# A two-layer hybrid decoder on one core: modulation sums by products with ones, a latent projection by quarters, and rotary halves exchanged by ScalarE copies

## The chip, the cores and the metric

The kernel runs on one core of one Trainium2 chip. The metric is the device time of one execution in microseconds (us); lower is better. The engines have these names in the profile: PE is TensorE (PEld its weight loads), DVE is VectorE, ACT is ScalarE, POOL is GpSimd, SP is SyncE, which here issues the DMAs.

## The reference: what is computed

A sequence of 256 rows of width 1024 passes two layers. Each layer is a token mixer and a SwiGLU feed-forward, both between RMS norms and modulated by shift, scale and gate vectors that come from one conditioning vector `c`:

```
c_act = jax.nn.silu(c)
for l in range(DEPTH):
    mod = c_act @ w_mod[l] + b_mod[l]
    sh_m, sc_m, g_m, sh_f, sc_f, g_f = jnp.split(mod, 6, axis=-1)
    h = rms_norm(x, mix_norm_pre[l]) * (1.0 + sc_m) + sh_m
    x = x + g_m * rms_norm(hybrid_mixer(h, ...), mix_norm_post[l])
    h = rms_norm(x, ffn_norm_pre[l]) * (1.0 + sc_f) + sh_f
    x = x + g_f * rms_norm(swiglu(h, ...), ffn_norm_post[l])
```

In the mixer one projection `h @ w_in` gives a latent of 256 columns (`cq`), attention keys and values, one index key, index weights, and the mLSTM parts. The normed latent is projected up to 8 query heads and 8 index-query heads of 64. An indexer scores all keys for each query, `sum_h w * relu(q_idx . k_idx)`, and only the 64 best causal keys take part in the softmax attention. A second head group is an mLSTM. Queries, keys, index queries and the index key are rotated:

```
x1, x2 = jnp.split(x, 2, axis=-1)
rope = concatenate([x1 * cos - x2 * sin, x2 * cos + x1 * sin], axis=-1)
```

The head width is 64, so each half has 32 elements, and the rotation needs the two halves exchanged.

## The kernel before, in words

Activations are held transposed: features on the 128 partitions, the 256 rows of the sequence along the free axis. The normed and modulated input of layer 0 is `n0hf` (8 blocks of 128 features), in full f32; from layer 1 on operands are split into two `fp32r` halves (names that end in `h` and `l`), and a product takes three passes.

**The prelude of layer 0.** The modulation vectors are matrix-vector products with 1024 x 6144 weights per layer (`w_mod`, 25 MB per layer). They are formed on DVE: `macc`, 128 partitions by n columns, gathers `w * c` over the 8 blocks of input features, and the sum over the partitions is left for PE. For the first norm the kernel does this by quarters q = 0..3 (`mod_quarter`): 8 loads of 256 KB each (tiles `wq`), 8 DVE operations of 128x512 (lines 206 and 208), then 4 PE transposes into a PSUM bank `pm`, a DVE reduce over it (line 218), an add of the bias (219), the scale vector `A` (220), two scalings that write two blocks of `n0hf` (line 965), and then the products `pvm` and `pva` of these two blocks, 16 of 128x512. Inside a quarter these steps are a chain, and PE waits on it.

**Mixer 0 after the prelude.** PE forms `m0pki` (index key, index weights and gates), `m0pcq` (the latent, 16 products), `m0kir` (rotated index key, by two products with the constant `dup`), `m0pwif`, `m0pgt` (gates), `m0pka` (attention keys), `m0pqidx` and `m0pq` (index queries, queries), the index scores `m0pi`, the logits `m0pl`. DVE rotates, computes the gates and the stabiliser scan `m0M`, goes on with the sums `macc` for the next modulation vectors (1 MB tiles `wm`, two 128x1024 operations each), adds up the scores `m0sc` and finds the 64th largest by rounds of MAX8 and MATCH_REPLACE8. ACT copies from PSUM, applies the relus `m0rl` and the exponentials. The first transposes of the attention weights, `m0pT`, need the exponentials, and these need the row maximum `m0mx`.

**Rotary.** `rope(dst, src, nm)` is called 6 times in each layer (names `rqidx0`, `rqidx1`, `rq0`, `rq1`, `rka0`, `rka1`), on a PSUM tile of 128 partitions (two heads of 64) by 512 columns:

```
xs = t2k(nm + "x"); copy(nm + "x", xs, src)         # ACT, PSUM to SBUF
pr = bankA(nm + "p"); matmul(pr, perm, xs)          # PE, halves exchanged and signed
dst = xs * cos                                       # POOL, or DVE
b = pr * sin; dst = dst + b                          # DVE (the add on POOL in two cases)
```

**Layer 1** has the same steps with three-pass products, with the later feed-forward blocks of PE work close behind. `row14p` are transposes that turn a gate vector into rows and do not belong to the rotary part.

**What sets the order.** The tile framework orders the instructions of each engine ahead of the run, by its own estimate of when each is ready; `issue_after` pins an operation behind another one. On the chip each engine then works through its list in that order, and an instruction that waits holds all behind it. SP issues the loads in order; SBUF tiles come from pools, and a load into a reused buffer waits for its last reader. PSUM banks come from two pools, `bankA` and `bankB`.

Of the kernel before, what the change touches and what calls it, by code (L numbers as in the profile page):

```python
# [56 lines left out]
def tile_hybrid_decoder(ctx: ExitStack, tc: tile.TileContext, a, out):  # L57
# [1006 lines left out]
```

## Time and profile before

| what | value |
|---|---|
| three runs | 734.39, 735.91, 737.62 us; median 735.91 us |
| the profiled execution, its own time | 736.93 us |
| span of the profiled execution | 735.2 us |
| PE busy | 702.1 us of it (95%) |
| DVE busy | 550.9 us (75%) |
| ACT busy | 348.3 us (47%) |
| POOL busy | 106.3 us (14%) |
| prelude, to the end of the last `pva` | about 58 us |
| mixer 0, from there to the first `m0pT` | about 60 us |
| from there to the start of layer 1's rotary part | about 306 us |
| layer 1's rotary part, to its first logits | about 40 us |

The span is counted from the first to the last instruction of the trace; the profiled execution has 1.73 us around it. Busy shares are averages over the program; the chain that ended last runs 80% through PE.

### The profile page before, as it was taken

Reading aid. Unit: us, or ns where it says so; the run is one execution under the profiler, and the core shown is the slowest. Engines: PE = TensorE matmul, PEld = TensorE weight load, DVE = VectorE, ACT = ScalarE, POOL = GpSimd, SP = SyncE. Lnnn points to the kernel's source line nnn. Section 1 sums busy time; section 2 is a strip of 40 time slices with the busy share of each in tenths; the row PEclk is TensorE's granted clock in tenths of the full one; section 3 lists DMA queues with packets and bytes.
Section 4 is the critical chain, followed back from the end, with each engine's and each line's share of the span. In section 5 each row is a group of like instructions: output and inputs, shape, how many; then the busy total and the mean of one; then the engine's idle time right before and its main releaser. Section 6 shows DMA issues by size and latency. Waiting matters only on the chain.

```text
span 735.2 us, 11619 instructions
## 1 busy us (share of the span) xinstructions
PE 702.1 (95%) x4581; PEld 618.8 (84%) x4581; DVE 550.9 (75%) x860; ACT 348.3 (47%) x613; POOL 106.3 (14%) x93
## 2 busy tenths in 40 slices
PE   2889999999999999999999989999999999999996
PEld 2337777888799999999988877999889999999995
DVE  4666989985998647897978899987776675655553
ACT  5112234665664444444536534685774444444442
POOL 1000420101000022210011263632210000000010
PEclk9999999999999999999999999999999999999999
DMA  9999953494958966989792933344536487664001
GB/s 305 355 297 386 367 208 104 159 329 156 315 211 303 332 217 230 339 295 340 257 370 90 329 118 115 121 150 131 181 135 228 164 303 260 215 207 172 1 1 57
DMA packets 106154, 162.77 MB, mean 221 GB/s; under 512 B 7586, under 2 KB 83950, under 8 KB 106100
## 3 DMA queue, kind: packets, MB, share of 16 engines
q1 hardware_dynamic: 106100, 162.04, 64.7%
q8 instruction: 36, 0.59, 0.3%
q14 instruction: 18, 0.15, 0.1%
HBM read 160.98 MB, written 1.05 MB: 220 GB/s over the span
## 4 chain that ended last, share of the span: by engine, by line
PE 80%; DVE 11%; ACT 3%; issue 3%; POOL 1%; DMA 1%; SPq 0%; DVEq 0%; POOLq 0%; ACTq 0%
PE f1pu L111 8%; PE f0pu L111 8%; PE f0pg L111 8%; PE f1pg L111 8%; PE f1y L111 7%; PE f0y L111 7%; PE m1pqk L111 3%; PE m1y L111 3%; PE pvm L111 3%; PE m0y L111 2%; PE pva L111 2%; PE m0pka L111 2%; PE m1pva L111 2%; PE m1pom L111 1%; PE m1pka L111 1%
## 5 line engine op out<-in xcount | busy, mean ns | idle before, releaser
L191 DVE SCALAR_TENSOR_TENSOR macc<-wm,ccol,macc 128x1024 f32<-128x1024 f32 x70 | 96.1, 1373 | 9.5 <-DMA wm<-in_w_mod_dram 8.8
L258 POOL TENSOR_TENSOR macc<-macc,br 1x512 f32<-1x512 f32 x6 | 10.0, 1666 | 166.6 <-DMA br<-in_b_mod_dram 166.6
L111 PE MATMUL m0pqk<-n0hf,m0wqk 128*128 128x256 f32 x128 | 29.6, 382 | 0.0
L111 PEld LDWEIGHTS m0pqk<-n0hf,m0wqk 128*128 128x128 f32 x128 | 23.8, 190 | 3.6 <-issue 0.5
L111 PE MATMUL pvm<-m0wvm,n0hf 128*128 128x512 f32 x32 | 18.5, 732 | 7.3 <-ACT n0hf L965 5.6
L208 DVE SCALAR_TENSOR_TENSOR macc<-wq,ccol,macc 128x512 f32<-128x512 f32 x28 | 21.0, 752 | 1.1
L111 PEld LDWEIGHTS pvm<-m0wvm,n0hf 128*128 128x128 f32 x32 | 7.1, 234 | 16.4 <-ACT n0hf L965 7.7
L965 ACT ACTIVATE n0hf<-n0xT,mod,A 128x256 f32<-128x256 f32 x7 | 3.9, 594 | 30.5 <-DVE A L220 30.5
L111 PE MATMUL m0pka<-n0hf,m0wka 128*128 128x256 f32 x64 | 16.0, 389 | 0.0
L111 PE MATMUL m0pom<-m0wom,n0hf 128*128 128x256 f32 x64 | 14.5, 379 | 0.0
L111 PE MATMUL pva<-m0wva,n0hf 128*128 128x512 f32 x32 | 14.4, 592 | 0.0
L111 PEld LDWEIGHTS m0pka<-n0hf,m0wka 128*128 128x128 f32 x64 | 11.5, 190 | 3.3 <-issue 1.6
L872 DVE TENSOR_TENSOR f1t<-f1pu,f1s 128x512 f32<-128x512 f32 x11 | 7.6, 692 | 7.5 <-PE f1pu L111 6.0
L111 PEld LDWEIGHTS m0pom<-m0wom,n0hf 128*128 128x128 f32 x64 | 11.9, 190 | 1.4
L262 POOL TENSOR_TENSOR ml<-macc,mh 128x512 fp32r<-128x512 f32 x6 | 9.5, 1586 | 24.0 <-ACT mh L260 24.0
L711 ACT ACTIVATE m0lm<-m0lm,m0mx 128x128 f32<-128x128 f32 (+1 forms) x16 | 7.1, 445 | 12.2 <-DVE m0mx L708 12.2
L111 PEld LDWEIGHTS pva<-m0wva,n0hf 128*128 128x128 f32 x32 | 6.1, 190 | 7.7 <-issue 7.7
L189 DVE TENSOR_SCALAR macc<-wm,ccol 128x1024 f32<-128x1024 f32 x10 | 8.8, 884 | 4.7 <-DMA wm<-in_w_mod_dram 3.5
L882 ACT CAST f0th<-f0t 128x512 fp32r<-128x512 f32 x10 | 6.2, 620 | 11.9 <-DVE f0t L872 11.9
L770 DVE SCALAR_TENSOR_TENSOR m1cv<-m1pqk,vc,m1cv 128x255 f32<-128x255 f32 (+2 forms) x24 | 11.1, 476 | 0.7 <-ACT m1cv L764 0.5
L218 DVE TENSOR_REDUCE mod<-pm 128x4 f32<-128x512 f32 x4 | 2.8, 692 | 11.8 <-PE pm L115 11.8
L115 PE MATMUL n0pt<-ident,n0xr 128*128 128x128 f32 x16 | 3.9, 428 | 7.6 <-ACT n0xr L317 7.6
(1823 smaller groups left out, 2782.2 us busy)
## 6 DMA issues: line engine op xcount, KB each, us to landing
wm<-in_w_mod_dram SPq DMA_DIRECT2D x40, 1024.0 KB
f0wd<-in_w_down_dram SPq DMA_DIRECT2D x11, 1024.0 KB
f1wd<-in_w_down_dram SPq DMA_DIRECT2D x11, 1024.0 KB
f0wg<-in_w_gate_up_dram SPq DMA_DIRECT2D x10, 1024.0 KB
f0wu<-in_w_gate_up_dram SPq DMA_DIRECT2D x10, 1024.0 KB
f1wg<-in_w_gate_up_dram SPq DMA_DIRECT2D x10, 1024.0 KB
f1wu<-in_w_gate_up_dram SPq DMA_DIRECT2D x10, 1024.0 KB
wq<-in_w_mod_dram SPq DMA_DIRECT2D x32, 256.0 KB
```

What stands on the lines that cost most here:

```text
L111: final["pe"] = nc.tensor.matmul(*args, **kw)
L115: final["pe"] = nc.tensor.transpose(*args)
L189: nc.vector.tensor_scalar_mul(acc, w[:, kk, :], ccol[:, k:k + 1])
L191: nc.vector.scalar_tensor_tensor(acc, w[:, kk, :], ccol[:, k:k + 1], acc, op0=ALU.mult, op1=ALU.add)
L208: last = nc.vector.scalar_tensor_tensor(acc, w[:, kk, :], ccol[:, k:k + 1], acc, op0=ALU.mult, op1=ALU.add)
L258: nc.gpsimd.tensor_tensor(acc[0:1, :], acc[0:1, :], br[0:1, :], op=ALU.add)
L262: nc.gpsimd.tensor_tensor(lo, acc, hi.bitcast(F32), op=ALU.subtract)
L711: final["exp"] = nc.scalar.activation(lm[:, g, :], lm[:, g, :], AF.Exp, bias=mx[:, g:g + 1], accum_out=den[:, hd:hd + 1])
L770: nc.vector.scalar_tensor_tensor(o[:, d:], s[:, :S - d], V["conv_w"][:, tap * 8 + j:tap * 8 + j + 1], o[:, d:], op0=ALU.mult, op1=ALU.add)
L872: nc.vector.tensor_mul(t, pu, s)
L882: nc.scalar.copy(th[:, 0], r3(t, 2))
L965: nc.scalar.activation(hf[:, j, :], s, AF.Identity, scale=A, bias=b)
```

## The change

There are two parts.

In the prelude, `mod_quarter` becomes `quarter_sums` and `quarter_mod`. The sum over partitions is done by 4 products with a column of ones (stationary `macc`, moving 128x1) instead of 4 transposes and a DVE reduce. The loads of a quarter are cut the other way (one k block and both halves each), 8 of 256 KB as before. The weight of the latent is loaded by quarters too (4 loads of 256 KB into one ring buffer), and the latent's 16 products are issued 4 at a time (`latent(q)`): three groups on PE between the ones products of a quarter and its `pvm`, the last behind the last `pva`. The first norm issues its squares first, then the scalings, transposes and copies. The constant `perm` is no longer loaded, and `freq` and `dup` hold other signs.

In `rope`, the product with `perm` is replaced by 4 ACT copies of 32 partitions by 512 each, from PSUM to SBUF, which exchange neighbouring groups of 32 partitions; the sign is in the sine table. DVE then reads `xw` in SBUF instead of `pr` in PSUM.

```
-    def mod_quarter(q):
+    def quarter_sums(q):
...
-            for kk in (0, 2):
-                for b in range(2):
-                    nc.sync.dma_start(raw.rearrange("p (k b n) -> p k b n", k=4, b=2)[:, kk:kk + 2, b, :],
-                                      src[:, 4 * t + kk:4 * t + kk + 2, b, q * 256:(q + 1) * 256])
             for kk in range(4):
                 k = 4 * t + kk
+                nc.sync.dma_start(raw.rearrange("p (k b n) -> p k b n", k=4, b=2)[:, kk], src[:, k, 0:2, q * 256:(q + 1) * 256])
...
+    def quarter_mod(q, acc):
         ps = bankA(f"pm0{q}")
         for j in range(4):
-            transpose(ps[:, j * P:(j + 1) * P], acc[:, j * P:(j + 1) * P], ident)
+            matmul(ps[:, j:j + 1], acc[:, j * P:(j + 1) * P], ones, start=True, stop=True)
...
-        nc.vector.tensor_reduce(out=m, in_=ps.rearrange("p (b j n) -> p b j n", b=2, j=2), axis=AX.X, op=ALU.add)
-        nc.vector.tensor_add(m, m, v)
+        nc.vector.tensor_add(m, r3(ps[:, 0:4], 2), v)
...
     def rope(dst, src, nm):
         xs = t2k(nm + "x")
         copy(nm + "x", xs, src)
-        pr = bankA(nm + "p")
-        matmul(pr, perm, xs, start=True, stop=True)
+        xw = t2k(nm + "w")
+        for p0 in range(0, P, 32):
+            nc.scalar.copy(xw[p0:p0 + 32, :], src[p0 ^ 32:(p0 ^ 32) + 32, :])
...
-        nc.vector.tensor_mul(r3(b, 2), r3(pr, 2), sb)
+        nc.vector.tensor_mul(r3(b, 2), r3(xw, 2), sb)
...
-        pcq = bankB(nm + "pcq")
-        feat(pcq, load_cols(win, C_CQ, nm + "wcq"), h, nm + "wcq", True, hf=hf)
+        pcq = pcq0
+        if l:
+            pcq = bankB(nm + "pcq")
+            feat(pcq, load_cols(win, C_CQ, nm + "wcq"), h, nm + "wcq", True)
...
+    rawcq = r3(ring.tile([P, 2048], F32, tag="raw", name="m0wcq"), 8)
+    pcq0 = bankA("m0pcq")
+
+    def latent(q):
+        for m in range(2):
+            for kk in range(2):
+                k = 2 * q + kk
+                matmul(pcq0[:, m * S:(m + 1) * S], rawcq[:, k, m * P:(m + 1) * P], hf[:, k, :],
+                       start=not (k or m), stop=k == KD - 1 and m == 1)
...
+        else:
+            with tc.issue_after(final["pe"].ins):
+                B = quarter_mod(q, acc)
+            with tc.issue_after(final["pe"].ins):
+                latent(q - 1)
...
+        nc.sync.dma_start(rawcq[:, 2 * q:2 * q + 2, :], a["w_in"][0][rows_q, C_CQ:C_CQ + 256].rearrange("(k p) n -> p k n", p=P))
...
+    with tc.issue_after(final["pe"].ins):
+        latent(3)
```

The order of instructions moves with it. On PE, behind the prelude in mixer 0 (`m0pki` is the index projection, `m0pgt` the gates, `m0pka` the keys), the list differs as follows, with - for before and + for the change:

```order
 L111 MATMUL m0pki<-n0hf,m0wsm 80x256 x8
-L111 MATMUL m0pcq<-n0hf,m0wcq 128x256 x16
 L111 MATMUL m0kir<-m0kix,dup 128x256 x2
 L115 MATMUL m0pwif<-ident,m0kix 128x80 x2
-L111 MATMUL m0pka_481<-n0hf,m0wka_437 128x256 x3
 L115 MATMUL m0pgt<-ident,m0wif 4x128 x4
-L111 MATMUL m0pka_481<-n0hf,m0wka_437 128x256 x13
-L111 MATMUL m0pqidx_504<-m0cqh,m0wup 128x256 x4
-L111 MATMUL m0pqidx_509<-m0cqh,m0wup 128x256 x4
-L111 MATMUL m0rqidx0p<-m0rqidx0x,perm 128x512
+L111 MATMUL m0pka_479<-n0hf,m0wka_435 128x256 x16
```

The latent is gone from this place, and the gate transposes `m0pgt`, which read `m0wif` from a DVE copy, now stand ahead of all 16 key products instead of behind three of them.

On DVE, at the same place, this stood in the list before (`macc` are the modulation sums, `m0kidx` and `m0kib` the rotated index key, `m0wif` the copy that `m0pgt` reads):

```order
L174 COPY vc_102<-pvec_380 128x74
L191 SCALAR_TENSOR_TENSOR macc_367<-wm_372,ccol,macc_367 128x1024 x2
L191 SCALAR_TENSOR_TENSOR macc_367<-wm_429,ccol,macc_367 128x1024 x2
L191 SCALAR_TENSOR_TENSOR macc_367<-wm_433,ccol,macc_367 128x1024 x2
L501 TENSOR_TENSOR m0kidx<-m0kir,cosT 128x256
L502 TENSOR_TENSOR m0kib<-m0kir,sinT 128x256
L508 COPY m0wif<-m0pwif 128x32
```

And this stands there in the change:

```order
L174 COPY vc_102<-pvec_397 128x74
L191 SCALAR_TENSOR_TENSOR macc_384<-wm_389,ccol,macc_384 128x1024 x2
L191 SCALAR_TENSOR_TENSOR macc_384<-wm_427,ccol,macc_384 128x1024 x2
L506 TENSOR_TENSOR m0kidx<-m0kir,cosT 128x256
L507 TENSOR_TENSOR m0kib<-m0kir,sinT 128x256
L191 SCALAR_TENSOR_TENSOR macc_384<-wm_431,ccol,macc_384 128x1024
L508 TENSOR_TENSOR m0kidx<-m0kidx,m0kib 128x256
L191 SCALAR_TENSOR_TENSOR macc_384<-wm_431,ccol,macc_384 128x1024
L513 COPY m0wif<-m0pwif 128x32
```

The index key moves two sums ahead; the copy `m0wif` keeps all six sums ahead of it.

On ACT, in layer 1's rotary part (`Mp` is a cast of the scanned stabiliser `m1M`, `row` copies belong to `row14p`), this stood before:

```order
L90 COPY m1rqidx0x<-m1pqidx_3946 128x512
L90 CAST m1wva01h<-m1wva_4126 128x1024
L90 COPY m1rqidx1x<-m1pqidx_3959 128x512
L528 CAST Mp<-m1M 4x256
L90 COPY m1rq0x<-m1pq_3999 128x512
L90 COPY m1rq1x<-m1pq_4020 128x512
L90 COPY row_4049<-row14p_4050 128x512
L90 COPY row_4049<-row14p_4056 128x512
```

And this stands there now:

```order
L90 COPY m1rqidx0x<-m1pqidx_3962 128x512
L354 COPY m1rqidx0w<-m1pqidx_3962 32x512 x4
L90 CAST m1wva01h<-m1wva_4154 128x1024
L90 COPY m1rqidx1x<-m1pqidx_3975 128x512
L354 COPY m1rqidx1w<-m1pqidx_3975 32x512
L533 CAST Mp<-m1M 4x256
L354 COPY m1rqidx1w<-m1pqidx_3975 32x512 x3
L90 COPY row_4077<-row14p_4078 128x512
L90 COPY m1rq0x<-m1pq_4018 128x512
L354 COPY m1rq0w<-m1pq_4018 32x512 x4
L90 COPY row_4077<-row14p_4084 128x512
L90 COPY m1rq1x<-m1pq_4042 128x512
```

Sixteen copies of 32 partitions stand among the ones that were there, three of them behind the cast `Mp`, and the PSUM bank that each group reads stays taken until its fourth copy.

## Rows read from the trace of the kernel before

**Rows 1.** The page: busy time, share of the span, instructions.
```profile
PE 702.1 (95%) x4581; PEld 618.8 (84%) x4581; DVE 550.9 (75%) x860; ACT 348.3 (47%) x613; POOL 106.3 (14%) x93
```

**Rows 2.** Timeline of PE, prelude: start, length, engine, line, operation, idle before.
```profile
15.84 1.11 PE L115 MATMUL pm<-ident,macc 128*128 128x128 f32 x4
18.82 5.69 PE L111 MATMUL pvm<-m0wvm,n0hf 128*128 128x512 f32 x8 [1.87 <-ACT n0hf L965]
...
30.19 3.70 PE L111 MATMUL pvm<-m0wvm,n0hf 128*128 128x512 f32 x8 [1.81 <-ACT n0hf L965]
...
39.63 5.40 PE L111 MATMUL pvm<-m0wvm,n0hf 128*128 128x512 f32 x8 [1.87 <-ACT n0hf L965]
```

**Rows 3.** The page's groups: DVE's reduce in the prelude.
```profile
L218 DVE TENSOR_REDUCE mod<-pm 128x4 f32<-128x512 f32 x4 | 2.8, 692 | 11.8 <-PE pm L115 11.8
```

**Rows 4.** Timeline of PE, mixer 0.
```profile
61.75 6.42 PE L111 MATMUL m0pcq<-n0hf,m0wcq 128*128 128x256 f32 x29
...
71.13 5.78 PE L111 MATMUL m0pka<-n0hf,m0wka 128*128 128x256 f32 x26
76.74 3.62 PE L111 MATMUL m0pqidx<-m0cqh,m0wup 128*128 128x256 f32 x16
80.20 1.02 PE L111 MATMUL m0rqidx0p<-m0rqidx0x,perm 128*128 128x512 f32 x2
81.06 0.95 PE L111 MATMUL m0pcs<-ones,m0sq 128*128 128x1 f32 x8
...
118.53 1.48 PE L115 MATMUL m0pT<-ident,m0lm 128*128 128x128 f32 x4 [0.66 <-ACT m0lm L711]
```

**Rows 5.** Timeline of DVE, mixer 0.
```profile
57.99 7.88 DVE L191 SCALAR_TENSOR_TENSOR macc<-wm,ccol,macc 128x1024 f32<-128x1024 f32 x6
69.34 0.42 DVE L501 TENSOR_TENSOR m0kidx<-m0kir,cosT 128x256 f32<-128x256 f32 x1 [3.46 <-PE m0kir L111]
...
81.88 0.68 DVE L356 TENSOR_TENSOR m0rqidx0b<-m0rqidx0p,sinT 128x512 f32<-128x512 f32 x1
...
91.01 1.26 DVE L357 TENSOR_TENSOR m0q<-m0q,m0rq1b 128x512 f32<-128x512 f32 x1
...
116.74 1.21 DVE L708 TENSOR_REDUCE m0mx<-m0lm 128x8 f32<-128x1024 f32 x1
```

**Rows 6.** Timeline of POOL, mixer 0: two of its rotary operations.
```profile
81.06 2.03 POOL L354 TENSOR_TENSOR m0qidx<-m0rqidx1x,cosT 128x512 f32<-128x512 f32 x1 [0.18 <-ACT m0rqidx1x L90]
...
90.45 1.27 POOL L357 TENSOR_TENSOR m0q<-m0q,m0rq0b 128x512 f32<-128x512 f32 x1 [1.83 <-DVE m0rq0b L356]
```

**Rows 7.** Timeline of ACT, mixer 0: latent's scaling, a gate step, two copies.
```profile
68.70 0.83 ACT L491 ACTIVATE m0cqh<-m0pcq,vc 128x256 f32<-128x256 f32 x2
72.68 0.41 ACT L521 ACTIVATE m0gc<-m0gc 4x256 f32<-4x256 f32 x1 [3.14 <-DVE m0gc L520]
...
86.46 0.59 ACT L90 COPY m0rq1x<-m0pq 128x512 f32<-128x512 f32 x1 [2.00 <-PE m0pq L111]
86.94 0.59 ACT L90 COPY m0rka0x<-m0pka 128x512 f32<-128x512 f32 x1
```

**Rows 8.** Busy time by stretch (PE, PEld, DVE, ACT, POOL; count), granted clock, DMA share, GB/s.
```profile
18.80:58.00 39.20, 33.79 (x79) 15.20 (x80) 25.73 (x49) 7.25 (x13) 0.00 (x0) 0.96 1.01 331
39.90:43.30 3.40, 3.40 (x5) 1.38 (x5) 3.22 (x6) 0.17 (x1) 0.00 (x0) 0.50 0.99 335
...
118.00:421.00 303.00, 298.08 (x2041) 273.46 (x2042) 249.51 (x348) 159.02 (x281) 32.94 (x26) 1.00 0.77 264
...
426.00:436.00 10.00, 7.77 (x41) 5.95 (x42) 9.72 (x12) 2.27 (x5) 9.01 (x5) 0.83 0.41 133
```

**Rows 9.** Timeline of PE, layer 1's rotary part.
```profile
432.58 2.07 PE L111 MATMUL m1rq0p<-m1rq0x,perm 128*128 128x512 f32 x2 [2.23 <-ACT m1rq0x L90]
434.45 1.74 PE L115 MATMUL row14p<-ident,A 128*128 128x128 f32 x8
```

**Rows 10.** Timeline of ACT, the same stretch.
```profile
431.64 0.40 ACT L528 CAST Mp<-m1M 4x256 fp32r<-4x256 f32 x1 [5.30 <-DVE m1M L526]
```

More of the change, by code (lines that the diff above doesn't have):

```diff
@@ L208, in mod_quarter @@
                     last = nc.vector.scalar_tensor_tensor(acc, w[:, kk, :], ccol[:, k:k + 1], acc, op0=ALU.mult, op1=ALU.add)
-        if q == 0:
-            with tc.issue_after(last.ins):
-                first()
+        return acc, last
+    def quarter_mod(q, acc):
         ps = bankA(f"pm0{q}")
         for j in range(4):
-            transpose(ps[:, j * P:(j + 1) * P], acc[:, j * P:(j + 1) * P], ident)
+            matmul(ps[:, j:j + 1], acc[:, j * P:(j + 1) * P], ones, start=True, stop=True)
         two = slice(2 * q, 2 * q + 2)
@@ L312, in first_norm @@
         xT = [work.tile([P, 4, S], F32, tag="big", name=f"{nm}xT{g}", bufs=4) for g in range(2)]
+        rs_ = [row_rms([xhalf(i, 0), xhalf(i, 1)], f"{nm}x{i}") for i in range(NT)]
+        pts = []
         for i in range(NT):
-            r = row_rms([xhalf(i, 0), xhalf(i, 1)], f"{nm}x{i}")
+            with tc.issue_after(final["rms"].ins):
+                xr = [t2k(f"{nm}xr{i}{g}") for g in range(2)]
+                for g in range(2):
+                    final["xr"] = nc.scalar.activation(xr[g], xhalf(i, g), AF.Copy, scale=rs_[i])
             for g in range(2):
-                xr = t2k(f"{nm}xr{i}{g}")
-                nc.scalar.activation(xr, xhalf(i, g), AF.Copy, scale=r)
                 ps = bankB(f"{nm}pt{i}{g}")
                 for j in range(4):
-                    transpose(ps[:, j * P:(j + 1) * P], xr[:, j * P:(j + 1) * P], ident)
+                    transpose(ps[:, j * P:(j + 1) * P], xr[g][:, j * P:(j + 1) * P], ident)
+                pts.append((i, g, ps))
+        with tc.issue_after(final["xr"].ins):
+            for i, g, ps in pts:
                 nc.scalar.copy(xT[g][:, :, i * P:(i + 1) * P], r3(ps, 4))
@@ L955, in tile_hybrid_decoder @@
     early = {n: [bankB(f"p{n}{i}") for i in range(NT)] for n in ("vm", "va")}
[L956 to L957 removed]
+    rawcq = r3(ring.tile([P, 2048], F32, tag="raw", name="m0wcq"), 8)
[6 more added lines that the diff above has]
+                       start=not (k or m), stop=k == KD - 1 and m == 1)
+    for q in range(4):
+        acc, last = quarter_sums(q)
+        if q == 0:
+            with tc.issue_after(last.ins):
+                first()
+            B = quarter_mod(q, acc)
+        else:
+            with tc.issue_after(final["pe"].ins):
+                B = quarter_mod(q, acc)
+            with tc.issue_after(final["pe"].ins):
+                latent(q - 1)
         wv = {n: r3(split.tile([P, 1024], F32, tag=t, name=f"m0w{n}{q}"), 2) for n, t in (("vm", "hi"), ("va", "lo"))}
+        rows_q = slice(q * 256, (q + 1) * 256)
         for name, c0 in (("vm", C_VM), ("va", C_VA)):
[L960 removed]
+            nc.sync.dma_start(wv[name], a["w_in"][0][rows_q, c0:c0 + 512].rearrange("(k p) n -> p k n", p=P))
+        nc.sync.dma_start(rawcq[:, 2 * q:2 * q + 2, :], a["w_in"][0][rows_q, C_CQ:C_CQ + 256].rearrange("(k p) n -> p k n", p=P))
         two = slice(2 * q, 2 * q + 2)
```

12 lines of the change are left out of this document (5 added, 7 removed).

## The prediction

> **What bounds the kernel now.** I read the profile's page first: PE is busy 95% of the span [rows 1]. That is an average, so I then looked, stretch by stretch, for places where PE isn't the one that sets the pace, and where the change reaches in. There are three. In the prelude PE waits in each quarter for the chain from `pm` to `n0hf`: 1.87, 1.81 and 1.87 us of idle are shown [rows 2]. One of these waits is followed by a fall of the granted clock: the stretch from 39.9 to 43.3 has 0.50 [rows 8], the lower level, 1.2 GHz, and `pvm` takes 5.40 us there and 3.70 a quarter earlier [rows 2]. So that fall costs 1.70 us.
>
> In mixer 0 PE is full up to 118, but it is not alone: there is little slack on DVE. The first transposes `m0pT` at 118.53 wait for ACT [rows 4], which waits for the row maximum `m0mx`, done at 117.95 [rows 5], behind all of DVE's top-k. Of DVE's idle time there, one long piece stands out: 3.46 us in front of `m0kidx`, until PE has done the latent and `m0kir` [rows 5]. What makes mixer 0 shorter must end `m0mx` earlier; it isn't enough that PE has less to do.
>
> From 118 to 421 PE is busy 298.08 of 303 us [rows 8]; what is won or lost ahead of it should pass through it unchanged. The third place is layer 1's rotary part: in 426 to 436 PE has 7.77 of 10 us, DVE 9.72 [rows 8]. PE waits 2.23 us for the copy `m1rq0x` [rows 9], which stands on ACT behind the cast `Mp`, and that waited 5.30 us for DVE's scan `m1M` [rows 10]. The clock fell again, and the product behind it took 2.07 us instead of 1.02 [rows 9, 4].
>
> **The prelude, step by step.** The reduce of 0.69 us [rows 3] goes from each quarter's chain. Four products with ones are of the kind of `m0pcs`, of which eight passes take 0.95 us [rows 4]; the transposes in their place took 1.11 us at half clock [rows 2]. In quarter 0 the chain runs from 15.84 to 18.82 and should lose about 1.2 us (the reduce, and half a microsecond for the first norm's order, an estimate; bounds 0.69 and 1.9). In the quarters behind it, four latent products fill the wait: a pass takes 6.42 / 29 = 0.22 us [rows 4], four products of two passes 1.77. They lie in an idle time of about 1.85 us. A quarter was 39.63 - 30.19 = 9.44 us, of which 1.87 idle [rows 2]; it becomes 7.57 + 1.77 and up to 0.5 for the dearer ones products at full clock, about 9.6. Three such quarters give back 0.5 to 0.7, the clock that no longer falls saves 1.70, and the last latent group behind the last `pva` costs 1.77. So the four terms nearly cancel, and `m0pki` begins within 0.2 us of where it did, but with the latent done. Behind `m0pki` the latent took 32 passes, 7.0 us [rows 4]. That is gone; in its place `m0kir` waits for ACT's copy of `m0pki`, at the price of a small ACT operation, 0.41 [rows 7]. So `m0kir` begins **about 6.5 us earlier on PE**, at 61.6 and not 68.1 (61.75 + 6.35).
>
> The loads: the DMA share is 1.01 at 331 GB/s in this stretch [rows 8], so 256 KB more in each quarter arrive about 0.8 us later per quarter, 2.4 us by the last. DVE, which takes them, is busy 25.73 of the 39.20 us [rows 8], so its sums have room and I cost this at nothing; without that cover it is 2.4 us. On SP's queue four loads of 256 KB stand earlier, and the 1 MB that they replace is gone behind them.
>
> **What is given back behind it.** The DVE list of the change has four sums in front of `m0kidx` and all six in front of the copy `m0wif`. A sum is 7.88 / 6 = 1.31 us [rows 5]. From 57.99: four sums to 63.2, two rotary products of at most 0.42 to 63.9, a sum, an add, a sum: 66.9 for `m0wif`. PE has done `m0kir` at about 63, and its next instruction is now `m0pgt`, which needs `m0wif`; all 16 key products queue behind it. So PE idles some 4 us, from 63 to 67. Then pgt 0.44 and 32 passes of 5.61 / 26 = 0.216 us [rows 4]: `m0pqidx` at 74.4 instead of 76.74, and with its length of 3.46 `m0pcs` at about 77.9 instead of 81.06, since the product at 80.20 is gone too. If the clock falls in that wait, 1.70 of this goes too.
>
> DVE now has `m0wif` at 66.9 instead of about 70.0 (69.34 and two products): 3.1 us of lead, nearly the 3.46 of idle that is gone. Of this I take off 0.3 for a wait for `m0pcs`, 0.6 for a longer wait for POOL's small power behind it (an estimate: POOL's rotary product ahead of it took 2.03 us [rows 6]), and 0.6 for `b`. That last one: `b = xw * sin` reads two tiles in SBUF; before, one operand was in PSUM. The trace shows the PSUM form beside POOL's 2.03 us product at 0.68 us [rows 5, 6], and an add with two SBUF operands beside POOL's work at 1.26 us (91.01, POOL from 90.45) [rows 5, 6]. So `b` is bounded by 0.68 and 1.26; six of them in a mixer cost between nothing and 3.5 us. I take one of the six at the upper bound, since most of POOL's products now end before their `b` begins (ACT's four copies come in between). Mixer 0: 3.1 - 0.3 - 0.6 - 0.6 = **1.6 us gained**, bounds +3.5 and -1.
>
> The Trainium skill, GPSIMD Engine Reference, section Key points, says that GpSimd shares its SBUF interfaces with VectorE and contends with VectorE instructions that have two SBUF inputs. The rows just named agree, 0.68 against 1.26; by that rule every `b` beside POOL would stand nearer 1.26, 0.58 us dearer, as in rival C.
>
> The copies on ACT: a copy of 128x512 is 0.59 us, two in a row start 0.48 apart [rows 7]. Fewer partitions don't shorten it: 4x256 takes 0.41 us, and two of 128x256 take 0.83 [rows 7]. So four copies of 32 partitions are bounded by 4 x 0.41 = 1.64 (256 columns, too low) and 4 x 0.59; I take 4 x 0.48 = 1.9 us for each rope, 23 us on ACT over the program. In mixer 0 ACT has room: 348.3 us busy in all [rows 1], and `m0cqh` and the gates are followed by idle. The products that they replace were 12 x 0.86 (80.20 to 81.06) = 10.3 us of PE [rows 4].
>
> **Layer 1.** There PE's place in the queue gets worse. `rqidx0p`, `rqidx1p`, `rq0p`, `rq1p` go from PE, but `row14p` needs the PSUM bank that the four copies of `rqidx1` hold, and three of these stand behind `Mp`, which still waits for DVE until 431.64 [rows 10]. From there: `Mp` to 431.95, three copies to 433.4, four transposes (half of 1.74 [rows 9]) to 434.3, a row copy to 434.8, `rq0x` and its four copies at 0.48 to 437.2, and then the bank is free for the second keys `m1pka`. They began behind `row14p` and `rq1p` (434.45, 1.6 and 0.86 us), thus at about 436.9. So 0.3 us later, and PE has only short transposes between 428.6 (432.58 less 2.23 and two products) and 437.2: the clock should be at the lower level, another 1.7 us. Then `rka0p` and `rka1p` are saved, 1.72. Sum: **0.3 us lost**, bounds 1.5 gained (clock not fallen) and 4 lost (a later `m1M`, and `b` at 1.26 us).
>
> Sum: -1.6 + 0.3 = -1.3 us. Against the profiled execution's own 736.93 that is 735.6; it lies 1.02 above the median of 735.91, so the median becomes 734.6. I say **734.6 us**, no change that can be told (0.5%, 3.7 us, is about what a measurement of this kernel can tell from none).
>
> **Rivals.** *A: all that PE saves comes through.* 10.3 us of products, 1.7 of clock, 1.2 in quarter 0 and the hidden latent, less what DVE must take: -9 to -12, 724 to 727 us. For it: PE's 95%. Against: both places where PE is relieved are places where it ends up waiting for DVE or ACT. 0.10.
>
> *B: part of it comes through.* PE's lead of 6.5 us brings DVE its 3.46, contention stays at 0.68 for `b`, and in layer 1 `m1pka` isn't held or the clock stays: -3.5 and -1.5, about 731. For it: the removed wait of 3.46 is a long one. 0.20.
>
> *C: `b` with two SBUF operands is slow throughout*, at the upper bound of [rows 5]: 12 x 0.58 = 7 us on DVE, 3.5 of it in mixer 0 where DVE sets the end, as much ahead of `m1M` in layer 1. From three slow `b` in mixer 0 on, the gain there is gone; with all, +2 to +5, about 739. 0.12.
>
> *D: ACT becomes the bound in layer 1.* `m1pka` waits for copies beyond 438.5 (two more copies, or a later `Mp`), with a cold clock, and in mixer 0 the wait of `m0pgt` makes the clock fall as well: +3.7 to +6, about 740.5. It decides from a start of `m1pka` 2 us later than before, relative to `m1pqidx`. 0.12.
>
> *E: the forecast*, within 3.7 us of before, 0.46.
>
> Faster is A and B, 0.30; slower C and D, most of it, 0.23; same 0.47. The range leaves out A and the upper part of D: 729 to 740; the forecast's own case runs from 732.2 to 739.6.
>
> **What the changed profile would show.** Right: `pvm` of quarter 2 at 3.7 us, `m0kir` near 62, an idle time of about 4 us in front of `m0pgt` ended by DVE, ACT copies of 32x512 at 0.5 us, `m0mx` at 115 to 118, `m1pka` behind `rq0w`, with a granted clock of 0.5. Wrong: if `m0mx` ends before 114, the DVE walk was too tight (A or B); if `b` shows over 1 us on the mean, C; if PE doesn't wait for DVE at `m0pgt`, the order was misread. A shift between 118 and 421 that is not the one at 118 would show something that I have not seen.

## The result and the profile after

The changed kernel takes 758.55 us (median of 4 runs, 756.68 to 761.68); the kernel before on the same chip 736.76 us (4 runs). The ratio is 1.0303, with a 95% interval of 1.0274 to 1.0332: slower by 3%. The forecast of 734.6 us and its range, 729 to 740, were wrong. The profiled execution has its own time of 761.68 us and a span of 760.0, 24.8 us more than before. It lies 3 us above its median, so the stretches below add up to more than the 21.8 us between the medians.

The page after, busy time and the granted clock in 40 slices (in tenths):

```profile
PE 712.5 (94%) x4573; PEld 631.9 (83%) x4573; DVE 548.4 (72%) x856; ACT 377.1 (50%) x661; POOL 107.7 (14%) x93
...
PEclk9998898999999999999999979999999999999999
```

PE has twelve products less, 10.3 us by the forecast, and yet is busy 10 us longer [rows 1]. The reason stands in the last line: a busy PE at the lower clock, 1.2 GHz, does less. To see where, I cut both traces at the same events of PE: the first `m0pki`, `m0pT`, `m0ca0p` (transposes of the attention output), `m1pqidx`, `m1pva`, `m1pT`, `m1y`. The rows give for each stretch the busy time of PE, PEld, DVE, ACT, POOL, the granted clock, the DMA share and GB/s. Before, from `m0pki` to `m1y`:

```profile
57.60:118.50 60.90, 60.27 (x280) 46.12 (x278) 51.68 (x109) 13.59 (x32) 14.52 (x15) 1.00 0.79 277
118.50:150.50 32.00, 31.43 (x192) 27.11 (x193) 29.03 (x56) 22.09 (x54) 2.96 (x2) 1.00 0.55 193
150.50:421.80 271.30, 267.45 (x1858) 247.15 (x1856) 220.19 (x292) 137.23 (x227) 30.78 (x24) 1.00 0.80 273
421.80:442.30 20.50, 18.27 (x122) 15.49 (x121) 19.21 (x28) 7.75 (x12) 12.40 (x7) 0.92 0.36 114
442.30:472.70 30.40, 30.40 (x215) 25.68 (x213) 29.41 (x78) 15.74 (x40) 14.38 (x13) 1.00 0.33 114
472.70:516.60 43.90, 43.90 (x379) 43.16 (x378) 34.45 (x76) 32.36 (x70) 14.04 (x7) 1.00 0.42 138
```

After, the same events:

```profile
58.00:122.40 64.40, 55.15 (x236) 42.37 (x234) 49.47 (x98) 27.79 (x57) 15.79 (x15) 0.87 0.79 279
122.40:160.00 37.60, 35.91 (x193) 30.75 (x194) 31.91 (x69) 21.52 (x52) 2.90 (x2) 0.87 0.42 154
160.00:431.60 271.60, 267.75 (x1858) 247.27 (x1856) 217.85 (x291) 137.15 (x226) 31.94 (x24) 1.00 0.80 272
431.60:456.70 25.10, 16.84 (x116) 15.84 (x114) 20.62 (x28) 17.00 (x28) 14.03 (x6) 0.80 0.42 133
456.70:488.80 32.10, 30.35 (x211) 26.50 (x209) 27.32 (x79) 21.38 (x48) 10.78 (x13) 0.95 0.18 64
488.80:541.00 52.20, 48.32 (x378) 46.25 (x377) 36.62 (x73) 33.29 (x70) 16.23 (x9) 0.93 0.37 124
```

I call the five stretches that changed A, B, C, D and E (the long one between B and C passes the shift on, 271.6 against 271.3). Idle is length less PE's busy time; time lost to the clock is estimated as (1 - granted clock) times the length, which is an upper estimate, since part of the time at the lower clock is idle.

- **A** is 3.5 us longer. Idle grew from 0.63 to 9.25, and 0.13 x 64.4 = 8.4 went to the clock, more than PE's shorter work gave back (six products gone, the latent now ahead of A). The clock stands at 0.50 from 64.3 to 71.1, around the wait for `m0wif`, and from 88.2 to 98.4, in the score stage.
- **B** is 5.6 us longer, with PE's work unchanged: 4.9 to the clock, 1.1 to idle.
- **C** is 4.6 us longer: idle 8.26 against 2.23, clock 5.0 against 1.6; four products less give some of that back.
- **D** is 1.7 us longer, with 1.75 of idle in front of logits that wait for the rotated keys `m1kT`. **E** is 8.3 us longer: idle is 3.88 where there was none, and 3.7 went to the clock.

The timeline of PE in the prelude and mixer 0, after (start, length; in brackets the idle time ahead and who ended it):

```profile
39.57 3.60 PE L111 MATMUL pvm<-m0wvm,n0hf 128*128 128x512 f32 x8
...
62.04 1.13 PE L111 MATMUL m0kir<-m0kix,dup 64*128 64x256 f32 x4 [0.46 <-ACT m0kix L90]
...
67.09 1.01 PE L115 MATMUL m0pgt<-ident,m0wif 128*4 128x128 f32 x4 [3.63 <-DVE m0wif L513]
67.90 8.66 PE L111 MATMUL m0pka<-n0hf,m0wka 128*128 128x256 f32 x32
...
88.30 1.22 PE L111 MATMUL m0pi<-m0kidx,m0qidx 64*128 64x128 f32 x4 [1.25 <-DVE m0qidx L360]
...
91.46 2.07 PE L111 MATMUL m0pi<-m0kidx,m0qidx 64*128 64x128 f32 x8
...
122.40 1.64 PE L115 MATMUL m0pT<-ident,m0lm 128*128 128x128 f32 x4 [3.44 <-ACT m0lm L716]
...
136.95 0.66 PE L115 MATMUL m0pT<-ident,m0lm 128*128 128x128 f32 x4 [1.01 <-ACT m0PT L90]
138.28 1.10 PE L111 MATMUL m0po<-m0va,m0PT 128*128 128x64 f32 x8 [0.67 <-ACT m0PT L90]
```

The prelude came as forecast: `m0kir` at 62.04 (forecast 61.6), then 3.63 us of idle in front of `m0pgt`, ended by DVE. The clock falls there, an "if" of the prediction that its sum leaves out: the 32 passes of `m0pka` take 8.66 us, where the forecast had 32 x 0.216 = 6.9. What was not forecast stands below it: PE, relieved of its products, waits 1.25 us for DVE's `m0qidx` in the score stage. Behind that wait eight small `m0pi` take 2.07 us. At 122.40 `m0pT` waits 3.44 us, where it waited 0.7 before [rows 4]. The clock is low again in B, and PE waits twice more there for ACT's copies `m0PT`; the order of ACT's and DVE's work in B is not that of before. DVE in mixer 0, after:

```profile
80.83 0.16 DVE L588 TENSOR_SCALAR m0rqm<-m0pcs 128x2 f32<-128x2 f32 x1 [2.39 <-PE m0pcs L111]
...
120.62 1.20 DVE L713 TENSOR_REDUCE m0mx<-m0lm 128x8 f32<-128x1024 f32 x1
```

ACT after, at the rope's copies, and in layer 1:

```profile
78.93 2.34 ACT L354 COPY m0rqidx0w<-m0pqidx 32x512 f32<-32x512 f32 x4
81.30 0.59 ACT L90 COPY m0rqidx1x<-m0pqidx 128x512 f32<-128x512 f32 x1
...
442.07 0.40 ACT L533 CAST Mp<-m1M 4x256 fp32r<-4x256 f32 x1 [2.44 <-DVE m1M L531]
442.50 1.75 ACT L354 COPY m1rqidx1w<-m1pqidx 32x512 f32<-32x512 f32 x3
446.56 2.34 ACT L354 COPY m1rq0w<-m1pq 32x512 f32<-32x512 f32 x4
```

Four copies of 32 partitions take 2.34 us, 0.585 each: they don't overlap, as two whole copies did at 0.48 from start to start [rows 7]. PE in layer 1, after:

```profile
444.31 1.11 PE L115 MATMUL row14p<-ident,A 128*128 128x128 f32 x4 [5.84 <-ACT m1rqidx1w L354]
...
448.95 0.58 PE L111 MATMUL m1pka<-nm0hh,m1wka10h 128*128 128x256 f32 x1 [1.74 <-ACT m1rq0w L354]
...
496.13 0.44 PE L115 MATMUL m1pT<-ident,m1lm 128*128 128x128 f32 x2 [1.74 <-ACT m1lm L716]
...
530.76 1.87 PE L111 MATMUL m1pqk<-m1cv,m1cv 128*128 128x256 f32 x8 [2.15 <-ACT m1cv L782]
```

The first wait is the forecast one: `row14p` behind `Mp` and three copies, then `m1pka` behind `rq0w`. The last two are in E and have another cause, on DVE and POOL after:

```profile
492.22 2.10 DVE L101 TENSOR_TENSOR m1wqk110l<-m1wqk,m1wqk110h 128x1024 fp32r<-128x1024 f32 x1
494.23 1.21 DVE L713 TENSOR_REDUCE m1mx<-m1lm 128x4 f32<-128x1024 f32 x1
...
527.30 2.30 DVE L751 TENSOR_TENSOR m1rd<-m1rd,m1ra1r 128x8 f32<-128x8 f32 x1 [1.32 <-POOL m1ra1r L276]
```

```profile
527.23 2.35 POOL L101 TENSOR_TENSOR m1wo001l<-m1wo,m1wo001h 128x1024 fp32r<-128x1024 f32 x1
```

DVE before, at the same two places:

```profile
474.97 1.22 DVE L708 TENSOR_REDUCE m1mx<-m1lm 128x4 f32<-128x1024 f32 x1
476.11 1.22 DVE L101 TENSOR_TENSOR m1wqk110l<-m1wqk,m1wqk110h 128x1024 fp32r<-128x1024 f32 x1
...
504.08 0.17 DVE L746 TENSOR_TENSOR m1rd<-m1rd,m1ra1r 128x8 f32<-128x8 f32 x1 [0.29 <-POOL m1ra1r L280]
```

`m1wqk110l` is the low half of a weight's split and has nothing to do with the rotation. In the list of before it stands behind the second `m1mx`, in the changed one ahead of it, so the row maximum comes 2.1 us late, the exponentials too, and PE's transposes wait. Later `m1rd`, 128x8 elements, takes 2.30 us; in the same place before it ran 0.17. It began 0.07 us behind a split on POOL and ended with it. `m1cv` stands behind it on DVE, and PE's `m1pqk` waits 2.15 us for that. The Trainium skill, GPSIMD Engine Reference, section Key points, says that GpSimd contends for its SBUF interfaces with VectorE instructions that have two SBUF inputs; this row agrees, 2.30 against 0.17 us.

### The profile page after: what moved, and what is told of

It is laid out like the page before. It is cut to its first block, busy times and chain, and to the rows that moved or that the text cites. A ratio compares the mean times of both kernels' runs of the same rounds, so it can differ in the third digit from the quotient of the medians.

```text
span 760.0 us, 11656 instructions
## 1 busy us (share of the span) xinstructions
PE 712.5 (94%) x4573; PEld 631.9 (83%) x4573; DVE 548.4 (72%) x856; ACT 377.1 (50%) x661; POOL 107.7 (14%) x93
## 4 chain that ended last, share of the span: by engine, by line
PE 76%; DVE 9%; issue 6%; ACT 5%; POOL 2%; DMA 1%; SPq 0%; POOLq 0%; DVEq 0%; ACTq 0%
PE f1pu L111 8%; PE f0pu L111 8%; PE f1pg L111 8%; PE f0pg L111 8%; PE f1y L111 7%; PE f0y L111 7%; PE m0pqk L111 3%; PE m1y L111 3%; PE pvm L111 2%; PE m0y L111 2%; PE m0pka L111 2%; PE pva L111 2%; PE m1pqk L111 2%; PE m1pka L111 2%; DVE macc L191 1%
## 5 line engine op out<-in xcount | busy, mean ns | idle before, releaser
L191 DVE SCALAR_TENSOR_TENSOR macc<-wm,ccol,macc 128x1024 f32<-128x1024 f32 x70 | 91.4, 1306 | 8.9 <-DMA wm<-in_w_mod_dram 8.1
L111 PE MATMUL m0pqk<-n0hf,m0wqk 128*128 128x256 f32 x128 | 32.1, 407 | 0.0
L111 PEld LDWEIGHTS m0pqk<-n0hf,m0wqk 128*128 128x128 f32 x128 | 26.2, 209 | 4.0
L111 PE MATMUL m0pka<-n0hf,m0wka 128*128 128x256 f32 x64 | 19.3, 454 | 0.0
L111 PEld LDWEIGHTS m0pka<-n0hf,m0wka 128*128 128x128 f32 x64 | 13.7, 226 | 3.9 <-issue 1.8
L775 DVE SCALAR_TENSOR_TENSOR m0cv<-m0pqk,vc,m0cv 128x255 f32<-128x255 f32 (+2 forms) x24 | 11.1, 475 | 1.9 <-ACT m0cv L769 1.9
L225 DVE TENSOR_REDUCE mod<-pm 128x4 f32<-128x512 f32 x14 | 9.2, 685 | 4.0 <-PE pm L115 4.0
L101 POOL TENSOR_TENSOR f0wd910l<-f0wd,f0wd910h 128x1024 fp32r<-128x1024 f32 x1 | 3.1, 3085 | 57.2 <-ACT f0wd910h L90 57.2
```

The costliest lines, as they stand in the source:

```text
L101: final["lo"] = (nc.gpsimd if aside != (name in OTHER) else nc.vector).tensor_tensor(lv, raw, hv.bitcast(F32), op=ALU.subtract)
L111: final["pe"] = nc.tensor.matmul(*args, **kw)
L225: nc.vector.tensor_reduce(out=m[:, 4 * g:4 * g + 4], in_=r3(ps, 4), axis=AX.X, op=ALU.add)
L775: nc.vector.scalar_tensor_tensor(o[:, d:], s[:, :S - d], V["conv_w"][:, tap * 8 + j:tap * 8 + j + 1], o[:, d:], op0=ALU.mult, op1=ALU.add)
```

## The experiments

"The whole change" is the changed kernel, "before" the kernel before. In the table, lengths of A to E in us in each profiled execution, and the median; ratio [95%] is to before on the same chip. The lengths can be off by 0.1. The profiled execution of e2_rope lies 6.6 us above its median. The runs are from several chips, on which before has medians of 735.5 to 737.4 us; a difference of two medians can carry that, a difference of two ratios does not.

```
kernel                        A     B     C     D     E    median  ratio
before                      60.9  32.0  20.5  30.4  43.9      -
p1_prelude                  60.1  32.0  20.7  30.3  43.9   735.14  0.9987 [0.9971, 1.0004]
e2_rope                     60.1  36.6  25.9  30.6  54.8   753.45  1.0255 [1.0215, 1.0296]
e3_copies_l0                59.2  36.7  20.8  30.4  43.9   738.86  1.0039 [1.0022, 1.0057]
e4_copies_l1                61.2  32.0  25.2  30.6  54.7   750.78  1.0197 [1.0170, 1.0225]
after                       64.4  37.6  25.1  32.1  52.2   758.55  1.0303 [1.0274, 1.0332]
e5_from_sbuf                61.2  37.7  19.5  34.2  47.1   748.60  1.0177 [1.0142, 1.0212]
e6_one_copy                 59.5  33.4  20.6  30.2  57.3   749.78  1.0191 [1.0155, 1.0226]
e7_fill_l1                  64.0  37.5  23.1  32.0  54.2   759.45  1.0317 [1.0287, 1.0346]
e8_copies_unread            60.0  32.3  23.8  31.4  51.7   749.05  1.0186 [1.0128, 1.0243]
e9_products_unread          61.8  32.3  23.0  31.4  49.9   746.75  1.0149 [1.0098, 1.0200]
e10_no_exchange             59.7  33.5  20.2  30.2  57.4   749.51  1.0184 [1.0136, 1.0231]
e16_no_exchange_pin         60.4  33.5  20.3  30.2  52.1   745.43  1.0108 [1.0089, 1.0127]
e15_no_exchange_pins        60.2  33.5  13.8  39.0  49.4   744.09  1.0107 [1.0081, 1.0134]
e12_pin                     64.8  37.7  24.9  32.1  45.1   752.30  1.0222 [1.0163, 1.0281]
e14_pins                    64.6  37.6  21.2  30.4  49.9   750.14  1.0179 [1.0158, 1.0200]
p2a                         70.6  32.0  20.7  30.3  43.9   747.37  1.0156 [1.0127, 1.0185]
p3_prelude_late             60.2  32.1  20.5  30.3  44.5   736.26  0.9980 [0.9968, 0.9993]
```

### Each part alone: p1_prelude, e2_rope, e3_copies_l0, e4_copies_l1

`p1_prelude` is the whole change with the products back (and `perm` and the signs with them); `e2_rope` is before with the copies alone; e3 and e4 choose by layer.

```
+        if nm[1] == "0":      # e3; "1" in e4; never in p1
             xw = t2k(nm + "w")
...
+        else:
+            xw = bankA(nm + "p")
+            matmul(xw, perm, xs, start=True, stop=True)
```

> The prelude part alone, rotary halves exchanged by products on PE as before. Theory T1 (the ACT copies are what PE comes to wait for, and each wait lets the granted clock fall): 731 to 737 us, no more than three stretches at half clock. Theory T2 (the gate transposes m0pgt, which now wait for DVE in mixer 0, start the loss): the stretch at half clock near 64 to 72 stays, and the time is 740 to 746 us.

> The rotary part alone, with the prelude as before. T1: nearly all of the loss is here, 752 to 760 us, with 8 or more stretches of 3.4 us at half clock. T2: 746 to 752 us, since the loss in mixer 0 stays away.

> The whole change, but layer 1 keeps the products on PE; only layer 0 has copies. From the shift of 9.6 us that the changed kernel shows between 170 and 410 us, both theories expect about 746 us; T1 that layer 1 has one stretch at half clock as before the change.

> The whole change, but layer 0 keeps the products on PE; only layer 1 has copies. T1: layer 0 is no slower than before the change and layer 1 loses its 15 us, 747 to 752 us. T2: the loss of mixer 0 stays as well, 755 us and more.

The prelude part costs nothing and may give 1 us: 735.14, first `m0pT` 1.6 us earlier than before, the wait there 0.78 us. The copies alone cost 2.55%. On top of p1 those of layer 0 add 3.7 us, those of layer 1 15.6; together they add 23.4, 4 us more than their sum. e3 is a miss: both theories had about 746 us for it, and it takes 738.86. Of layer 1's, C takes 4.5 and E, where the list moved, some 11. And e3 has the same operations in layer 0 as the whole change in another list: A is 59.2 there, not 64.4.

### What in the copies costs: e5_from_sbuf, e6_one_copy, e10_no_exchange

e5 reads the copy in SBUF, so that the PSUM bank comes free after one copy. e6 makes one copy of 128 partitions (the exchange is left out); e10 has neither copy nor product, `b` reads `xs` (left out too).

```
-            nc.scalar.copy(xw[p0:p0 + 32, :], src[p0 ^ 32:(p0 ^ 32) + 32, :])
+            nc.scalar.copy(xw[p0:p0 + 32, :], xs[p0 ^ 32:(p0 ^ 32) + 32, :])   # e5
+        nc.scalar.copy(xw, src)                                                # e6, for the loop
```

> The whole change, but the four copies of 32 partitions read the SBUF copy x instead of PSUM, so that the PSUM bank is free after one copy. Theory L (the length of the copies on ACT is what PE waits for): 755 to 765 us, since a copy from SBUF isn't shorter. Theory H (the bank that is held until the fourth copy is what stops PE, in layer 1 row14p and m1pka): at least 5 us come back, 745 to 753 us, and row14p no longer waits behind the cast Mp.

> The whole change, but each rope has one copy of 128 partitions instead of four of 32; the exchange of the halves is left out by this, everything else runs. Theory L: 735 to 740 us. Theory H: the same, since the bank is held for one copy only. Theory P (b with two SBUF operands is slow beside POOL): 745 us and more, since b still reads SBUF.

> The whole change with neither product nor copy: b reads the plain copy x (the exchange of the halves is left out). This is what the rotary part could give at best. Theory L: 727 to 732 us. Theory D: 742 to 752 us, no better than with one copy.

The bank held by the copies is a real cost, as theory H had it: e5 gives 10 us back (C 19.5, E 47.1), though four copies from SBUF take longer, 2.50 us. With one copy (e6) or no exchange at all (e10) the kernel still takes 1.9 and 1.8% more than before, but in another place. A, B and C together are then 113.5 and 113.4 us long, before 113.4, in the whole change 127.1. The loss is in E alone, and the two marks of the list stand there too: the split ahead of `m1mx`, and `m1rd` at 2.30 us. So what lengthens A, B and C needs the four copies; what lengthens E does not, and what e10 shares with the whole change there is a list made anew. The time of e6 is also in the range of theory P (`b` with two SBUF operands is slow), but the ropes stand in A, C and D, which are no longer than before.

### Load without use: e8_copies_unread, e9_products_unread

e8 is p1 with the 48 copies added and nobody reading them; e9 the whole change with the products kept, unread.

```
+        pr = bankA(nm + "p")
+        matmul(pr, perm, xs, start=True, stop=True)      # e9
```

> The prelude part with the products on PE, used as before, and beside them the 48 copies on ACT, whose result nobody reads. This prices the copies as load alone (2.34 us of ACT in each rope, and a PSUM bank held for it), with PE's work kept. Theory L (the time of the copies on ACT): 748 us and more. Theory D (PE without the products runs dry next to a DVE that is full, its clock falls, and a list of orders made anew puts other work in front of what PE waits for): 735 to 742 us.

> The whole change, the copies used, and beside them the products on PE kept without a reader: 10.3 us of PE work that does nothing but occupy it. Theory L: 758 to 765 us. Theory D: less than the whole change in spite of the added work, 740 to 752 us, with fewer us at half clock than 50.6.

Theory D had e9 right and e8 wrong: 735 to 742 us were expected of e8, and its 749.05 lies where theory L had it. Useless products make the changed kernel some 12 us *faster* (758.55 to 746.75), and useless copies make p1 some 14 us slower.

In e9 A and B shrink from 102.0 to 94.1, with the clock at 1.00 through B. It isn't the absence of the products alone that costs the difference, since e10, which has neither products nor copies, takes 93.2 for A and B. The lists tell more. Seven runs lose in B, with 36.6 to 37.7 us: e2, e3, e5, e7, e12, e14 and the whole change, all with four copies and without products in layer 0. They share one order of ACT's and DVE's work in B. In all other runs B takes 32.0 to 33.5 us, and ACT's order there is that of before, in e9 and e10 too. And in A the four traces with 64.0 to 64.8 us (the whole change, e7, e12, e14) have the same lists of PE and DVE, which no other run has. No run pins one of these orders, so how much of A and B is the order, and how much the copies' time beside a PE with less work, is not shown.

What stays in E is of a list again. ACT in e9, PE's wait behind it, and ACT before:

```profile
514.96 0.60 ACT L828 ACTIVATE m1og<-m1pom 128x512 f32<-128x512 f32 x1
515.58 1.28 ACT L784 ACT_TABLE_LOAD   x1
516.87 0.63 ACT L784 ACTIVATE m1cv<-m1cv 128x512 f32<-128x512 f32 x1
```

```profile
517.55 1.57 PE L111 MATMUL m1pqk<-m1cv,m1cv 128*128 128x256 f32 x8 [2.29 <-ACT m1cv L784]
```

```profile
506.63 0.63 ACT L777 ACTIVATE m1cv<-m1cv 128x512 f32<-128x512 f32 x1
...
508.57 0.60 ACT L821 ACTIVATE m1og<-m1pom 128x512 f32<-128x512 f32 x1
```

In e9, as in e8, ACT takes `m1og` ahead of `m1cv`, with a load of tables of 1.28 us between them; before, `m1cv` came first. PE in e8, at the worst place:

```profile
482.09 1.47 PE L111 MATMUL m1po<-m1va,m1PT 128*128 128x64 f32 x8 [3.25 <-ACT m1PT L90]
```

That copy `m1PT` stands in e8's list behind four exponentials which wait for `m1mx`; before, both copies stood ahead of them. The split stands where it was in e8 and e9, and `m1rd` takes 0.17 us, so these are other ways to lose E.

### The order itself: e12_pin, e14_pins, e16_no_exchange_pin, e15_no_exchange_pins

e12 is the whole change with `m1wqk110l` pinned behind the second `m1mx`; e14 pins the cast `Mp` of layer 1 behind the last rope copy as well. e16 and e15 are the same two on e10.

```
+        with tc.issue_after(final["m1mx10"].ins) if name == "m1wqk110" else ExitStack():
             final["lo"] = (nc.gpsimd if aside != (name in OTHER) else nc.vector).tensor_tensor(lv, raw, hv.bitcast(F32), op=ALU.subtract)
...
+            with tc.issue_after(final["rope"].ins):     # e14, e15
+                store_M()
```

> The whole change, with one DVE operation of layer 1 pinned back to where it stood before: the low half m1wqk110l behind the second row maximum m1mx instead of in front of it. If orders made anew carry a share of the loss (theory D): the wait of PE ahead of m1pT near 494 goes, with the half clock behind it, 2 to 6 us less, 752 to 757 us. If orders don't matter: 758 us.

> The whole change with two operations of layer 1 pinned: m1wqk110l behind the second m1mx, and the cast Mp behind the last rotary copy. Theory D: the 5.84 us wait ahead of row14p shrinks by 2 us and more, 746 to 751 us. If the length of ACT's copies sets that wait: no better than with the first pin, 752 us.

> Neither product nor copy, with m1wqk110l alone pinned behind the second m1mx. Theory D: 6 us less as in the whole change, 742 to 745 us; the rest is the wait ahead of the second row14p, behind Mp.

> Neither product nor copy (the exchange is left out), with the same two operations pinned. Theory D: most of the loss against the prelude part alone goes, 733 to 742 us, where without the pins it was 749.5. If the loss lies in the missing PE work itself: 746 to 749 us.

DVE in e12:

```profile
491.22 1.22 DVE L714 TENSOR_REDUCE m1mx<-m1lm 128x4 f32<-128x1024 f32 x1
492.36 1.22 DVE L102 TENSOR_TENSOR m1wqk110l<-m1wqk,m1wqk110h 128x1024 fp32r<-128x1024 f32 x1
...
520.30 0.17 DVE L752 TENSOR_TENSOR m1rd<-m1rd,m1ra1r 128x8 f32<-128x8 f32 x1 [0.29 <-POOL m1ra1r L277]
```

The pin of one instruction takes E from 52.2 to 45.1 and the median down 6.3 us, and `m1rd` is at 0.17 again. It isn't that one place alone: with the pin the framework also put other work of E back into the order of before, PE's next transposes, `m1wom10l` on DVE and `m1cv` on ACT among it. So the 7.1 us are the price of E's list, not of one split. On e10 the same pin (e16) gives 5 us of E, and 4 us by the medians, 5.6 by the ratios; 745.43 is just above the 742 to 745 expected. The second pin shortens C, 24.9 to 21.2, but E is 49.9 there, and 2.2 us are left of it. e15 lies between its two expectations (733 to 742, 746 to 749): C falls to 13.8, yet PE then waits in D:

```profile
460.65 0.71 PE L112 MATMUL m1pl<-m1kT,m1q 64*128 64x128 f32 x4 [3.26 <-POOL m1kT L358]
...
464.27 2.08 PE L112 MATMUL m1pl<-m1kT,m1q 64*128 64x128 f32 x12 [2.91 <-DVE m1kT L358]
```

Its first `m1pT` is at 474.5, before at 472.7. The second pin moves the wait and doesn't remove it: C and D together take 52.8 us in e15, 50.5 in e16 without that pin, 50.9 before.

### PE's own work and the clock: e7_fill_l1, p2a, e17_p2a_fill, p3_prelude_late

e7 is the whole change with the products `m1pq` of the second pair formed four times. p2a is p1 with two of the sums given to DVE a step later. e17 is p2a with the product `m0rq1p` formed five times. p3 is p1 with `Mp` of layer 1 pinned behind the last rope copy.

```
-                for m in range(2):
+                for m in [0, 1] * (4 if l and which and g else 1):             # e7
-    HEAD = ((2, 2, 1, 1), (3, 2, 1, 0, 0))
+    HEAD = ((2, 1, 2, 1), (3, 2, 1, 0, 0))                                     # p2a
+        for _ in range(5 if nm == "m0rq1" else 1):                             # e17
             matmul(pr, perm, xs, start=True, stop=True)
```

> The whole change, but layer 1 forms the second query bank m1pq four times over (same result), which fills 4.6 of the 5.84 us in which PE waits ahead of row14p. If the fall of the granted clock is a cause of its own: fewer us at half clock between 443 and 454 (10.2 without this) and 2 to 5 us less, 753.5 to 756.5 us. If the waits alone cost the time and the clock only accompanies them: 758 us or more.

> The prelude part alone, with one of the six sums' loads given out a step later in layer 0, so that DVE's copy m0wif stands behind four sums instead of six and PE isn't held at m0pgt. If the 4 us wait and the half clock at 65 to 70 are what ate the prelude's gain: 730 to 733 us. If the top-k on DVE bounds mixer 0 anyway: 734 to 736 us, as the prelude part alone.

> The slow variant of the prelude part (the sums given out a step later, 747.4 us, in whose score stage m0pi the granted clock stays at half for 27 us), with 3.4 us of work more on PE: the product m0rq1p is formed five times over ahead of that stage (same result), in the time in which PE waits three times. If the clock is a cause by itself: the stage m0pi runs at the full clock, and with more work the kernel is 8 to 13 us faster, 735 to 740 us. If the waits and the order cost the time and the clock only goes with them: 747 us or more.

> The prelude part alone, and in layer 1 the cast Mp moved behind the last rotary copy on ACT; nothing else moves but a neighbour on DVE. If the place of one operation in a list is worth microseconds (theory D): PE's wait of 2.2 us for m1rq0x goes, and the stretch at half clock behind it, 2 to 4 us less than the prelude part alone, 731 to 733.5 us, better than before the change. If lists don't matter: 735 us.

In e7 the fill did its work in C (23.1 instead of 25.1, clock 0.93 instead of 0.80), but E is 2 us longer, and the median, 759.45, missed the 753.5 to 756.5 that was expected. p2a removes the wait at `m0pgt` and loses 10 us of A for it; no more than 736 us were expected. Stretches of p2a:

```profile
76.00:86.00 10.00, 6.94 (x29) 4.40 (x27) 9.37 (x13) 1.66 (x3) 5.05 (x4) 1.00 1.08 366
86.00:113.00 27.00, 26.59 (x61) 16.68 (x62) 16.66 (x42) 6.25 (x15) 5.64 (x7) 0.51 0.47 164
```

and of e17, the same stretches:

```profile
76.00:86.00 10.00, 10.00 (x41) 6.85 (x40) 9.37 (x12) 1.66 (x3) 9.12 (x6) 1.00 1.07 370
86.00:113.00 27.00, 26.98 (x125) 18.91 (x124) 23.99 (x70) 6.73 (x16) 7.11 (x10) 1.00 0.68 235
```

In p2a PE is idle 3 of 10 us and then works through the whole score stage at 0.51, half the instructions in the same 27 us. With 3.4 us of useless products in front, the stage runs at 1.00 in the profiled execution. But not in every run: of e17's ten runs four lie at 734.7 to 739.0 us with a mean clock of 0.990 to 0.995, as the profiled one (736.67), and six at 745.5 to 749.2 with 0.973 to 0.978; the median is 746.12, between the two expectations (735 to 740, 747 or more), and the ratio 1.003 [0.9987, 1.0073] compares mostly the former. One program, 11 us apart, and what differs in the records is the clock. p2a's five runs, 745.5 to 749.6 us, all lie where the second group does; with so few runs it isn't shown that the fill made the first group likelier. The framework had also moved two sums, two passes of `m0pqk` and a few neighbours in e17, so the fill isn't the sole difference to p2a.

p3 was to gain 2 to 4 us on p1 and gained none: C takes 20.5 us against 20.7, and `m1pva` is at 441.8 against 441.0. It is 0.2% faster than before; p1's 0.1% isn't clear of noise, and the two can't be told apart.

## Why the prediction was wrong

**The prelude: right.** `pvm` of the third quarter takes 3.60 us instead of 5.40, the fall of the clock at 39.9 is gone, `m0kir` starts at 62.04, and PE idles 3.63 us for `m0wif`. The four terms of its sum add up to some 0.5 us earlier and not to nearly nothing; `m0pki` came 0.4 later (58.0 against 57.6). Alone (p1) the prelude part moves the first `m0pT` by 1.6 us, the size of the forecast's gain in mixer 0. That the sizes agree is partly luck: 0.6 of what the forecast takes off there is for `b`, which p1 leaves as it was.

**The copies: mis-sized.** 1.9 us for each rope were forecast, 2.34 measured. That is nearly the upper bound (4 x 0.59); I took 0.48 because whole copies start that far apart.

**`b` with two SBUF operands: mis-sized, but not the cause.** In mixer 0 the six took 0.68, 1.75, 0.69, 1.03, 0.88 and 0.69 us; 1.75 lies above the upper bound. That is 1.6 us more than six times 0.68, where 0.6 was priced. In layer 1 none took more than 0.75. Rival C was not the cause.

**Mixer 0, "1.6 us gained": failed.** DVE's lead came, `m0pgt` starts at 67.09. But the wait for `m0pcs`, priced at 0.3, was 2.39 us, since the clock had fallen behind the wait for `m0wif`; `b` cost 1.6 and not 0.6; and the 10.2 us of the score stage at the lower clock had no term at all. `m0mx` is done at 121.8, not between 115 and 118. I carried DVE's lead of 3.1 us to `m0mx` and priced only what stood on that path. I did not ask whether PE, with four copies on ACT in place of its six products, would keep the clock, nor what order the framework would make behind the edit. By the estimate above A and B lost 8.4 and 4.9 us to the clock. The missing products alone don't do this (e10).

**Layer 1, "0.3 us lost, bounds 1.5 gained and 4 lost": failed, in C by size, in E by kind.** The place was right (`row14p`, then `m1pka` behind `rq0w`, at the lower clock: rival D), but `m1pka` began 448.95 - 431.6 = 17.4 us behind `m1pqidx`, where the forecast had 15.1 (436.9 - 421.8). That meets the sign that the prediction gave for rival D, 2 us later; D's price of 3.7 to 6 us for the whole was too low all the same. C alone lost 4.6 us.

**"What is won or lost ahead of it should pass through it unchanged" was right from 160 to 431 us, and wrong for B, as it was for D and E, which I took over unchanged.** These are terms put at nothing without a reason. The shift of 3.9 us at `m0pT` was 9.5 behind B, which the prediction had named as the sign of something not seen. In B, D and E the framework's lists were made anew by its estimate of readiness, and in E a split came in front of the row maximum. I had compared the lists where the change reaches in and not behind. E cost 8.3 us: e12 shows that 7.1 of these go with its list.

Open stays how much of A and B is the changed order, and how much of the last 8 us of e15 is the wait for the keys and how much the clock. Why the clock stays low through a stage in which PE hardly waits, as in p2a, no run showed; the slower group of e17's runs has no trace.

## What to carry to other kernels

Taking work from a busy engine is a gain only if its neighbours in line can follow. Where what replaces it is slower and holds a buffer that the busy engine needs next, the relief turns into waits, and here the clock was lower behind several of them. Compare the changed order of instructions on every engine as far as the next long stretch that passes shifts on, not only at the edit, and look for foreign work that has come ahead of what the bound engine waits for. And price small partition-wise copies at the full time of one operation each.

## What was not expected of the hardware

The copies of 32 partitions cost 0.585 us each, while whole copies of 128 partitions start 0.48 us apart. A DVE operation of 0.17 us took 2.30 behind a POOL split of 2.35. And a stage with PE busy 26.59 of 27 us stayed at half the granted clock in one program, and ran at 1.00 with 3.4 us of extra products ahead of it in the one execution that was traced; six of ten runs of that program were some 11 us slower, at a lower mean clock.
